# Eight copies of v move from SyncE's to GpSimd's queue, a split of expert weights waits for a gather's issue, and indices are computed before affinities

## The chip, the cores and the metric

The kernel runs on one core of a Trainium2 chip. The metric is the device time of one execution in microseconds (us), the median of several runs. All times in the trace are counted from the start of the profiled execution's span.

## What is computed

A two-layer encoder runs over two sequences, a sample of 512 tokens and a prompt of 256, each of width 1024, in float32. A layer is

```
x = x + token_mixer(rmsnorm(x, norm1), w_in, rpb, gain_na, gain_dil, w_out)
x = x + expert_choice_ffn(rmsnorm(x, norm2), w_router, w_gate, w_up, w_down)
```

The mixer projects x by `w_in` to queries, keys and values of 16 heads of 64. The first four heads are neighborhood attention on a grid of 64 columns: a token of the sample sees 8 rows by 16 columns of keys around it. The other twelve are dilated attention in three patterns. Their outputs are normalised and multiplied by `w_out`.

The feed-forward part is routed by expert choice: `aff = softmax(x @ w_router)`, and each of 16 experts takes its top tokens (64 of the sample, 32 of the prompt), with their affinities `g` and indices `idx`:

```
xe  = x[idx]
ye  = (silu(xe @ w_gate) * (xe @ w_up)) @ w_down * g
y   = zeros.at[idx].add(ye)
```

After two layers a last rmsnorm gives the outputs.

## The kernel before, in words

**Products.** Every large product is made of three products on TensorE: each float32 operand is split into a high part `hi` (rounded by a copy on ScalarE) and a low part `lo` (the rest, a subtraction on VectorE), and hi*hi, hi*lo and lo*hi are summed in PSUM.

**The stream of weights.** `Stream` (L186) loads weights in a fixed order (`prefetch`, L201, a DMA on SyncE's queue, SP, at L209) and splits them in the same order (`convert`, L212: ScalarE's copy at L222 or L225, VectorE's subtraction at L223 or L226, where L222 and L223 are for the query weights, which are scaled). A raw buffer is loaded again when the split that reads it is done: w_in has two raw buffers, the expert weights a ring of 16 quarters of 1 MB.

**The order of the work.** The mixer (`Mixer`) is a set of generators. A planner (`Order` with `Clock`, a cost model of each engine) runs them when the kernel is built and fixes the order in which instructions are put into each engine's queue. Each engine then runs its own queue in order; SP's and POOL's (GpSimd's) queues are such queues too, and a DMA that waits for its data holds up those behind it. The change leaves the planner's costs and the order of the work as they are.

**The start of a layer.** `project` (L765) goes through the units of w_in: first the values of heads 0 to 3, then queries and keys of heads 0 and 1, and so on. The values of a row block of 128 tokens (products L818 to L820) go from PSUM to `y` (L825 on ScalarE, L826 on VectorE). Neighborhood attention of the sample needs v sorted by blocks of 16 columns instead of by rows, so for the first unit the four row blocks of the sample are stored to a DRAM buffer `blocks` (L829, four stores of 256 KB) and, when all four are in DRAM, loaded from it in the other order into `v` (L833, four loads of 256 KB). All eight are issued on SP. Products L788 to L790 are the projections of queries and keys, whose results L755 (ScalarE) and L761 (VectorE) split. L776 clears halves of the key buffers by memsets on GpSimd. L899 and L900 are the scores, L960 and L962 the products with v. `rstd` (L301) takes the power -0.5 on GpSimd (L307). `tables` and `prompt_tables` load attention biases on SP (L849, L856).

**Routing and the first expert.** `choose` finds each expert's top tokens; `choice` (L439) turns them so that each expert is a column and merges two halves: `m` says which half wins, `gT` becomes the affinities, `iT` the indices as integers, `iL` the last expert's indices again. Then `experts` (L316) begins. `gather(e)` (L328) is an indirect DMA on GpSimd (L330) that fetches the 96 rows of expert e from `table` in DRAM by the indices `iT`. Two gathers are issued, a further weight load is made to wait for the second, and `ws.convert(first + 3)` splits the second and third quarter of the first expert's gate weights (the first was split in the mixer). `flip` (L334) turns the gathered rows on TensorE (L340) and splits them (L342 on ScalarE, L343 on VectorE). Then the products run (L357), twelve for each quarter of a weight matrix.

Of the kernel before, what the change touches and what calls it, by code (L numbers as in the profile page):

```python
# [8 lines left out]
F32 = mybir.dt.float32  # L9
# [3 lines left out]
OP = mybir.AluOpType  # L13
# [41 lines left out]
class Clock:  # L55
# [3 lines left out]
    def __init__(self):  # L59
        self.at = dict.fromkeys(("pe", "act", "dve", "pool", "dma"), 0.0)  # L60
# [122 lines left out]
                self.tasks.remove(best)  # L183


class Stream:  # L186

    def __init__(self, nc):  # L190
        self.nc = nc
        self.load, self.parts, self.ready, self.turns = [], {}, {}, {}
        self.loaded = self.split = 0
        self.clock = Clock()
# [17 lines left out]
    def convert(self, n):  # L212
        nc = self.nc
        while self.split < min(n, len(self.load)):
            g = self.split
            while self.load[g][6] is None:
                self.prefetch(self.loaded + 1)
            _, _, size, hi, lo, ahead, w, arrival, _, scale = self.load[g]
            hi = hi([128, size * (1 if lo else 2)], F32R, name="hi")
            hi, lo = (hi, lo([128, size], F32R, name="lo")) if lo else (hi[:, :size], hi[:, size:])  # L220
            if scale:
                nc.scalar.activation(hi, w, AF.Copy, scale=scale)  # L222
                nc.vector.scalar_tensor_tensor(lo, w, scale, hi.bitcast(F32), op0=OP.mult, op1=OP.subtract)  # L223
            else:
                nc.scalar.activation(hi, w, AF.Copy)  # L225
                nc.vector.tensor_sub(lo, w, hi.bitcast(F32))  # L226
            self.ready[g] = self.clock.dve(size, self.clock.act(size, arrival))
            self.parts[g] = (hi, lo)
            self.split += 1
            self.prefetch(g + 1 + ahead)  # L230
# [6 lines left out]
class Kernel:  # L237
    def __init__(self, ctx, tc, a):
        self.tc, self.nc, self.a = tc, tc.nc, a
        nc = self.nc  # L240
        self.mem = ctx.enter_context(tc.tile_pool(name="mem", bufs=1, reuse_waits="tile"))
        self.pp = ctx.enter_context(tc.tile_pool(name="ps", bufs=2, space=bass.MemoryType.PSUM, reuse_waits="tile"))
        self.dram = ctx.enter_context(tc.tile_pool(name="dram", bufs=1, space=bass.MemoryType.DRAM))
        ctx.enter_context(tc.manual_schedule())
        self.zones = {}
        self.const = ctx.enter_context(tc.tile_pool(name="const", bufs=1))
        self.ident = self.const.tile([128, 128], F32, name="ident")
        nc.scalar.dma_start(self.ident, a["ident"])
        self.half = self.const.tile([128, 16], F32, name="half")
        nc.gpsimd.memset(self.half, -0.5)  # L250
        self.gcol = self.const.tile([128, DEPTH, KT], F32, name="gcol")
        nc.gpsimd.dma_start(self.gcol, a["gains"])
        self.wr = self.const.tile([128, DEPTH, KT, EXPERTS], F32, name="wr")
        nc.gpsimd.dma_start(self.wr, a["w_router"])
        g2 = self.const.tile([128, DEPTH, KT], F32, name="g2")
        nc.gpsimd.dma_start(g2, a["norm2_cols"])
        self.g2 = g2
        top = self.region(TOP_AT)
        self.top = top.tile([48, 2, CAP], F32, name="top")
        self.both = top.tile([CAP, 2, 2, EXPERTS], F32, name="both")  # L260
        self.pick = top.tile([CAP, 2, EXPERTS], F32, name="pick")
        self.iota = self.const.tile([CAP, 128], F32, name="iota")
        nc.scalar.dma_start(self.iota, a["iota"])
        self.flip = self.const.tile([CAP, CAP], F32, name="flip")
        nc.scalar.dma_start(self.flip, a["flip"])

        self.half_at = self.const.tile([CAP, 2], F32, name="half_at")
        for s, x in ((slice(0, CAP_S), (SS // 2, SS // 2)), (slice(CAP_S, CAP), (SP // 2, SS + SP // 2))):
            for c in range(2):
                nc.gpsimd.memset(self.half_at[s, c:c + 1], float(x[c]))  # L270
        self.gT = self.const.tile([CAP, EXPERTS], F32, name="gT")
        self.iT = self.const.tile([CAP, EXPERTS], U32, name="iT")
        self.iL = self.const.tile([CAP, 1], F32, name="iL")
        self.xres = self.dram.tile([NTOK, D], F32, name="xres")
        self.table = self.dram.tile([NTOK, D], F32, name="table")
        self.blocks = self.dram.tile([SS, 512], F32R, name="blocks")
        self.ws = Stream(nc)


    def zone(self, name, dtype):  # L280
# [35 lines left out]
    def experts(self, l, first):  # L316

        nc, ws, gT, iT = self.nc, self.ws, self.gT, self.iT
# [44 lines left out]
            return [self.bank(t)[:CAP] for t in tags]  # L363

        gather(0)
        gather(1)
        if ws.loaded < first + len(RING) + 1:
            ws.prefetch(ws.loaded + 1)
            self.tc.add_manual_dep(ws.dma.ins, gathers[1].ins.name, mybir.DependencyInfo(
                mybir.DependencyClass.Sync, mybir.DependencyReason.SCHED_ONLY), reason="rows before more weights")  # L370
            ws.prefetch(first + len(RING) + 1)
        ws.convert(first + 3)
        xT[0] = flip(xe[0], "x")
# [65 lines left out]
    def choice(self):  # L439


        nc, E = self.nc, EXPERTS
        p = self.bank("tp")[:CAP, :128].rearrange("p (v h c) -> p v h c", v=2, h=2)
        for v in range(2):
            nc.tensor.transpose(p[:, v].rearrange("p h c -> p (h c)")[:, :48], self.top[:, v], self.ident[:48, :48])
        t = self.both
        nc.vector.tensor_copy(t, p[:, :, :, :E])
        q = self.bank("tp")[:CAP, :2 * E].rearrange("p (v c) -> p v c", v=2)
        nc.tensor.matmul(q, self.flip, t[:, :, 1], start=True, stop=True)
        self.busy(BUSY[3])  # L450
        m, d = self.pick[:, 0], self.pick[:, 1]
        nc.vector.tensor_tensor(m, t[:, 0, 0], q[:, 0], op=OP.is_ge)
        nc.vector.tensor_tensor(self.gT, t[:, 0, 0], q[:, 0], op=OP.max)
        nc.vector.scalar_tensor_tensor(d, t[:, 1, 0], self.half_at[:, 0:1], q[:, 1], op0=OP.subtract, op1=OP.subtract)
        nc.vector.tensor_mul(d, d, m)
        nc.vector.scalar_tensor_tensor(self.iT, d, self.half_at[:, 1:2], q[:, 1], op0=OP.add, op1=OP.add)
        nc.vector.scalar_tensor_tensor(self.iL, d[:, E - 1:], self.half_at[:, 1:2], q[:, 1, E - 1:], op0=OP.add, op1=OP.add)


# [121 lines left out]
class Mixer:  # L581
# [183 lines left out]
    def project(self):  # L765

        nc, clock, ws = self.nc, self.clock, self.ws
        for n, (kind, i) in enumerate(UNITS):
# [30 lines left out]
            else:  # L799
# [8 lines left out]
                for t in range(TILES):  # L808
                    if t == 2:
                        ws.convert(c + 3)  # L810
                    s = slice(t * 128, (t + 1) * 128)
                    yield lambda: max(self.avail("pj"), ws.ready[c + 1], self.hT_at.get(t, NEVER))
                    hT = self.hT
                    p, b = self.bank("pj")
                    p = p[:, :256]
                    for k, (hi, lo) in enumerate(w):
                        at = clock.pe(768, max(ws.ready[c + 1], self.hT_at[t]))
                        nc.tensor.matmul(p, hT[0][:, k, s], hi, start=k == 0, stop=False)  # L818
                        nc.tensor.matmul(p, hT[0][:, k, s], lo, start=False, stop=False)  # L819
                        nc.tensor.matmul(p, hT[1][:, k, s], hi, start=False, stop=k == KT - 1)  # L820
                        if k < KT - 1:
                            yield lambda: 0.0
                    pv = p.rearrange("p (h d) -> p h d", h=4)
                    y = rows if t < SS // 128 else v
                    nc.scalar.activation(y[:, t, :, 0, :], pv, AF.Copy)  # L825
                    nc.vector.tensor_sub(y[:, t, :, 1, :], pv, y[:, t, :, 0, :].bitcast(F32))  # L826
                    self.free["pj"][b] = at = clock.dve(256, clock.act(256, at))
                    if near and t < SS // 128:
                        nc.sync.dma_start(self.k.blocks[s].bitcast(F32), y[:, t].rearrange("p h a d -> p (h a d)").bitcast(F32))  # L829
                    if near and t == SS // 128 - 1:  # L830
                        src = self.k.blocks.rearrange("(r b c) x -> b r c x", **GRID)
                        for b in range(GRID["b"]):
                            nc.sync.dma_start(v[:, b].rearrange("p h a d -> p (h a d)").bitcast(F32), src[b].bitcast(F32))  # L833
                        blocks_at = clock.dma(2048, at + 2.0)
                if near:
                    at = max(at, blocks_at)
# [503 lines left out]
```

## Time and profile before

| | us |
|---|---|
| median of 3 runs | 2063.65 |
| lowest and highest run | 2063.26, 2066.0 |
| profiled execution | 2064.48 |
| span of the profiled execution | 2062.7 |
| mean granted clock of TensorE | 0.986 |
| TensorE busy | 1983.1 (96% of the span) |
| VectorE, ScalarE, GpSimd busy | 1587.0, 1350.5, 210.7 |

PE is TensorE's matmul, PEld its weight load, DVE is VectorE, ACT ScalarE, POOL GpSimd; a q behind a name is the engine's queue, and SPq is SyncE's. In rows, L226 is line 226 of the kernel, `hi<-data,hi` is what an instruction writes and reads, and `[8.61 <-DVE heads L761]` says that the engine was idle for 8.61 us before it and which instruction ended that. The names are those of memory zones: `heads`, `data`, `turned` and `turned_lo` hold many things in turn. A granted clock of 1.00 is 2.4 GHz, 0.50 is 1.2 GHz.

### The profile page before, as it was taken

How to read it: one execution, taken by the hardware profiler on the slowest of the kernel's cores; microseconds unless marked ns; L12 is line 12 of the kernel's file. 1: busy time of each engine (PE TensorE's matmuls, PEld its weight loads, DVE VectorE, ACT ScalarE, POOL GpSimd, SP SyncE). 2: the span in 40 equal slices, each digit the busy share in tenths (PEclk: the TensorE clock that was granted, in tenths of full speed). 3: DMA queues.
4: the chain of work that ended last, by engine and by line, in shares of the span. 5: the costliest groups of instructions: out<-in, count | busy, mean ns of one | idle time of the engine just before them, and what ended most of it. 6: DMA issues, size and time to landing. Idle time of an engine off the chain costs nothing.

```text
span 2062.7 us, 27876 instructions
## 1 busy us (share of the span) xinstructions
PE 1983.1 (96%) x10602; PEld 1557.3 (76%) x10602; DVE 1587.0 (77%) x1978; ACT 1350.5 (65%) x1743; POOL 210.7 (10%) x149
## 2 busy tenths in 40 slices
PE   6999999989999999999979999999899999999997
PEld 6898898876777777777678998978667777777774
DVE  4566677767888888888846666777688888888887
ACT  4566666427777777777636666663377777777775
POOL 2000000010101010101010000000101010101011
PEclk9999999999999999999989999999999999999999
DMA  6212214679999999999352221246799999999974
GB/s 214 92 57 84 76 57 154 241 235 361 370 389 385 390 385 388 387 386 354 126 171 77 76 79 57 86 181 235 252 346 382 394 377 401 373 397 376 397 283 140
DMA packets 97142, 526.67 MB, mean 255 GB/s; under 512 B 11536, under 2 KB 14864, under 8 KB 47856
## 3 DMA queue, kind: packets, MB, share of 16 engines
q1 hardware_dynamic: 84320, 493.39, 62.8%
q0 software_dynamic: 7200, 25.06, 5.0%
q10 hardware_dynamic: 5488, 6.45, 1.3%
q8 instruction: 83, 1.36, 0.3%
q14 instruction: 51, 0.42, 0.1%
HBM read 485.79 MB, written 32.77 MB: 251 GB/s over the span
## 4 chain that ended last, share of the span: by engine, by line
PE 86%; DVE 5%; ACT 3%; DMA 2%; issue 2%; SPq 0%; ACTq 0%; POOL 0%; POOLq 0%; DVEq 0%
PE pj L357 17%; PE s L357 17%; PE av L357 8%; PE o L357 8%; PE pj L1082 5%; PE pj L788 3%; PE pj L789 3%; PE pj L790 3%; PE tp L932 3%; PE pj L818 2%; PE tp L340 2%; PE pj L820 2%; PE pj L819 2%; PE s L1082 2%; PE av L960 2%
## 5 line engine op out<-in xcount | busy, mean ns | idle before, releaser
L225 ACT ACTIVATE hi<-data 128x2048 fp32r<-128x2048 f32 (+1 forms) x170 | 289.5, 1703 | 61.3 <-PE s L357 24.6
L226 DVE TENSOR_TENSOR hi<-data,hi 128x2048 fp32r<-128x2048 f32 (+1 forms) x106 | 197.9, 1867 | 50.7 <-ACT hi L225 50.1
L357 PE MATMUL pj<-hi,parts 128*96 128x512 f32 x880 | 233.7, 393 | 2.8 <-DVE parts L343 2.3
L357 PE MATMUL s<-turned_lo,parts 128*96 128x512 f32 x872 | 221.7, 393 | 0.0
L908 ACT ACTIVATE data<-data 128x256 f32<-128x256 f32 (+1 forms) x192 | 119.1, 621 | 155.6 <-DVE data L906 147.5
L788 PE MATMUL pj<-turned,hi 128*128 128x256 f32 (+1 forms) x512 | 180.8, 353 | 17.8 <-DVE heads L761 16.5
L357 PEld LDWEIGHTS pj<-hi,parts 128*96 128x96 f32 x880 | 141.6, 161 | 64.7 <-DVE parts L343 3.2
L357 PEld LDWEIGHTS s<-turned_lo,parts 128*96 128x96 f32 x872 | 140.4, 161 | 60.7 <-DVE turned_lo L226 0.4
L357 PE MATMUL pj<-turned_lo,parts 128*96 128x512 f32 x656 | 181.6, 400 | 0.0
L789 PE MATMUL pj<-turned_lo,hi 128*128 128x256 f32 (+1 forms) x512 | 174.6, 341 | 0.0
L790 PE MATMUL pj<-turned,hi 128*128 128x256 f32 (+1 forms) x512 | 174.4, 341 | 0.0
L225 ACT ACTIVATE hi<-heads 128x2048 fp32r<-128x2048 f32 x80 | 152.8, 1913 | 32.4 <-PE s L357 20.4
L226 DVE TENSOR_TENSOR turned_lo<-data,hi 128x2048 fp32r<-128x2048 f32 x64 | 146.7, 2293 | 29.6 <-ACT hi L225 28.2
L357 PE MATMUL s<-hi,parts 128*96 128x512 f32 x664 | 169.0, 392 | 0.0
L226 DVE TENSOR_TENSOR turned_lo<-data,turned_lo 128x2048 fp32r<-128x2048 f32 (+1 forms) x68 | 151.4, 2226 | 19.3 <-ACT turned_lo L225 17.6
L405 POOL DMA_INDIRECT xres<-heads,iT x30 | 53.7, 1791 | 916.6 <-ACT heads L404 916.6
L225 ACT ACTIVATE turned_lo<-data 128x2048 fp32r<-128x2048 f32 (+1 forms) x68 | 127.0, 1868 | 30.0 <-PE pj L357 14.5
L357 PEld LDWEIGHTS s<-hi,parts 128*96 128x96 f32 x664 | 107.1, 161 | 46.3
L937 DVE TENSOR_TENSOR parts<-tp,parts 128x512 fp32r<-128x512 f32 (+2 forms) x160 | 99.6, 647 | 51.0 <-ACT parts L936 49.3
L357 PE MATMUL av<-hi,parts 128*96 128x512 f32 x400 | 134.5, 397 | 3.7 <-DVE hi L226 3.7
L357 PEld LDWEIGHTS pj<-turned_lo,parts 128*96 128x96 f32 x656 | 105.2, 164 | 42.9 <-ACT parts L342 0.5
L906 DVE CUSTOM_DVE_ANT_0 data<-s,data 128x512 f32<-128x512 f32 (+2 forms) x176 | 98.7, 579 | 28.9 <-PE s L900 27.2
(172 smaller groups left out, 4514.7 us busy)
## 6 DMA issues: line engine op xcount, KB each, us to landing
data<-in_w_up SPq DMA_DIRECT2D x70, 1024.0 KB, 8.7
data<-in_w_gate SPq DMA_DIRECT2D x66, 1024.0 KB, 8.1
data<-in_w_down SPq DMA_DIRECT2D x56, 1024.0 KB, 8.9
heads<-in_w_down SPq DMA_DIRECT2D x44, 1024.0 KB, 8.8
heads<-in_w_gate SPq DMA_DIRECT2D x42, 1024.0 KB, 7.6
heads<-in_w_up SPq DMA_DIRECT2D x34, 1024.0 KB, 9.7
turned<-in_w_down SPq DMA_DIRECT2D x28, 1024.0 KB, 8.9
turned<-in_w_up SPq DMA_DIRECT2D x24, 1024.0 KB, 7.0
```

The source lines that it names most:

```text
L225: nc.scalar.activation(hi, w, AF.Copy)
L226: nc.vector.tensor_sub(lo, w, hi.bitcast(F32))
L357: nc.tensor.matmul(ps[b], y[:, k, :], a[:, o:o + 512], start=k == 0 and w == 0, stop=k == KT - 1 and w == 2)
L405: nc.gpsimd.indirect_dma_start(out=self.xres, out_offset=bass.IndirectOffsetOnAxis(ap=iT[:, e:e + 1], axis=0), in_=y, in_offset=None, comp ...
L788: nc.tensor.matmul(p, hi[:, k, :], hT[0][:, k, s], start=k == 0, stop=False)
L789: nc.tensor.matmul(p, hi[:, k, :], hT[1][:, k, s], start=False, stop=False)
L790: nc.tensor.matmul(p, lo[:, k, :], hT[0][:, k, s], start=False, stop=k == KT - 1)
L906: nc.vector.tensor_tensor_reduce(out=x[:, j, :w], in0=p[:, j, :w], in1=tab[:, o:o + w], scale=-1.0, scalar=3.0e38, op0=OP.add, op1=OP.min, ...
L908: nc.scalar.activation(x[:, j, :w], x[:, j, :w], AF.Exp, bias=m, scale=-1.0, accum_out=self.den[n][:, t, a:a + 1])
L932: nc.tensor.transpose(p[:, a * S + t * 128:a * S + (t + 1) * 128], w[:, o:o + 128], self.k.ident)
L937: nc.vector.tensor_sub(lo[:, c], p[:, c], hi[:, c].bitcast(F32))
L1082: nc.tensor.matmul(p, y[:, i], z[:, b * 512:(b + 1) * 512], start=i == 0 and w == 0, stop=i == len(ks) - 1 and w == 2)
```

## The change

The eight copies of v by blocks are issued on GpSimd's queue instead of SP's. After the issue of the first gather GpSimd also clears one element of a new tile `mark`, and the next subtraction of `convert` (L226) has a dependency on that memset, as a wait on a semaphore. `gT` is computed after `iT` instead of right after `m`. The existing dependency between the second gather and a weight load is written by the new helper `order` and stays the same.

```diff
+def order(tc, later, sooner, reason):
+    tc.add_manual_dep(later.ins, sooner.ins.name, mybir.DependencyInfo(
+        mybir.DependencyClass.Sync, mybir.DependencyReason.SCHED_ONLY), reason=reason)
...
                 nc.scalar.activation(hi, w, AF.Copy)
-                nc.vector.tensor_sub(lo, w, hi.bitcast(F32))
+                x = nc.vector.tensor_sub(lo, w, hi.bitcast(F32))
+                if self.behind is not None:
+                    order(self.tc, x, self.behind, "rows asked for before VectorE is busy")
+                    self.behind = None
...
+        self.mark = self.const.tile([1, 1], F32, name="mark")
...
         gather(0)
+        ws.behind = nc.gpsimd.memset(self.mark, 0.0)
         gather(1)
...
         nc.vector.tensor_tensor(m, t[:, 0, 0], q[:, 0], op=OP.is_ge)
-        nc.vector.tensor_tensor(self.gT, t[:, 0, 0], q[:, 0], op=OP.max)
         nc.vector.scalar_tensor_tensor(d, t[:, 1, 0], self.half_at[:, 0:1], q[:, 1], op0=OP.subtract, op1=OP.subtract)
         nc.vector.tensor_mul(d, d, m)
         nc.vector.scalar_tensor_tensor(self.iT, d, self.half_at[:, 1:2], q[:, 1], op0=OP.add, op1=OP.add)
+        nc.vector.tensor_tensor(self.gT, t[:, 0, 0], q[:, 0], op=OP.max)
...
                     if near and t < SS // 128:
-                        nc.sync.dma_start(self.k.blocks[s].bitcast(F32), y[:, t].rearrange("p h a d -> p (h a d)").bitcast(F32))
+                        nc.gpsimd.dma_start(self.k.blocks[s].bitcast(F32), y[:, t].rearrange("p h a d -> p (h a d)").bitcast(F32))
                     if near and t == SS // 128 - 1:
                         src = self.k.blocks.rearrange("(r b c) x -> b r c x", **GRID)
                         for b in range(GRID["b"]):
-                            nc.sync.dma_start(v[:, b].rearrange("p h a d -> p (h a d)").bitcast(F32), src[b].bitcast(F32))
+                            nc.gpsimd.dma_start(v[:, b].rearrange("p h a d -> p (h a d)").bitcast(F32), src[b].bitcast(F32))
```

## Rows read from the trace of the kernel before

**Rows 1.** The page, section 4: engines' shares of the chain that ended last.
```profile
PE 86%; DVE 5%; ACT 3%; DMA 2%; issue 2%; SPq 0%; ACTq 0%; POOL 0%; POOLq 0%; DVEq 0%
```

**Rows 2.** Waits of TensorE, whole span: us in total, times, longest us.
```profile
PE pj L788 <- DVE heads L761: 16.5, 2, 8.6
...
PE tp L340 <- DMA heads<-table,iT: 9.9, 2, 5.3
PE av L357 <- DVE hi L226: 3.7, 2, 1.9
```

**Rows 3.** Timeline of TensorE, layer 0: start, duration, line, names, shapes [idle before].
```profile
37.48 0.40 PE L788 MATMUL pj<-turned,hi 128*128 128x512 f32 x1
...
54.59 0.77 PE L788 MATMUL pj<-turned,hi 128*128 128x512 f32 x1 [8.61 <-DVE heads L761]
...
89.91 0.42 PE L960 MATMUL av<-parts,heads 128*128 128x384 f32 x1
```

**Rows 4.** The chain of waits in order of time, layer 0: start, us, what.
```profile
33.59 5.71 DMA blocks<-heads
...
42.31 8.32 DMA data<-in_w_in
...
66.55 0.47 PE pj L788
```

**Rows 5.** Timeline of VectorE, layer 0.
```profile
24.95 1.23 DVE L223 SCALAR_TENSOR_TENSOR hi<-data,hi 128x1024 fp32r<-128x1024 f32 x1 [0.46 <-ACT hi L222]
...
27.29 1.28 DVE L678 SCALAR_TENSOR_TENSOR data<-data 128x1024 f32<-128x1024 f32 x1
```

**Rows 6.** Stretches: each engine's busy us (instructions), granted TensorE clock, DMA share, GB/s.
```profile
55.00:60.00 5.00, 5.00 (x13) 3.84 (x13) 1.56 (x2) 0.00 (x0) 0.00 (x0) 0.50 0.45 156
```

**Rows 7.** Timeline of TensorE, layer 1.
```profile
1075.76 0.77 PE L788 MATMUL pj<-turned,hi 128*128 128x512 f32 x1 [7.90 <-DVE heads L761]
...
1087.38 0.47 PE L788 MATMUL pj<-turned,hi 128*128 128x512 f32 x1 [0.47 <-ACT heads L755]
```

**Rows 8.** The chain of waits in order of time, layer 1.
```profile
1063.50 8.35 DMA data<-in_w_in
```

**Rows 9.** Timeline of VectorE, layer 1.
```profile
1047.82 1.23 DVE L223 SCALAR_TENSOR_TENSOR hi<-data,hi 128x1024 fp32r<-128x1024 f32 x1 [0.20 <-ACT hi L222]
```

**Rows 10.** Timeline of all engines at the first gather, layer 0.
```profile
451.31 0.23 DVE L456 SCALAR_TENSOR_TENSOR iT<-data,half_at,tp 96x16 uint32<-96x16 f32 x1
...
452.45 4.53 POOL L330 DMA_INDIRECT heads<-table,iT  x1 [11.29 <-issue]
453.78 2.28 DVE L226 TENSOR_TENSOR turned_lo<-heads,hi 128x2048 fp32r<-128x2048 f32 x1
457.29 0.96 POOL L330 DMA_INDIRECT heads<-table,iT  x1 [0.30 <-issue]
...
460.15 1.51 PE L340 MATMUL tp<-ident,heads 96*128 96x96 f32 x8 [4.52 <-DMA heads<-table,iT]
...
465.31 3.39 PE L357 MATMUL pj<-hi,parts 128*96 128x512 f32 x14
```

**Rows 11.** Timeline of all engines at the first gather, layer 1.
```profile
1473.30 4.55 POOL L330 DMA_INDIRECT heads<-table,iT  x1 [11.26 <-DVE iL L457]
...
1481.84 1.51 PE L340 MATMUL tp<-ident,heads 96*128 96x96 f32 x8 [5.33 <-DMA heads<-table,iT]
...
1483.29 4.92 PE L357 MATMUL pj<-turned_lo,parts 128*96 128x512 f32 x12
...
1488.05 3.39 PE L357 MATMUL pj<-hi,parts 128*96 128x512 f32 x14
```

**Rows 12.** The loads of w_in, all 48: from issue to landing.
```profile
DMA to landing us min/median/max: 3.2/4.6/9.0
```

**Rows 13.** Timeline of GpSimd, layer 0.
```profile
23.11 1.46 POOL L307 TENSOR_TENSOR data<-data,half 128x1 f32<-128x1 f32 x1 [1.33 <-DVE data L305]
24.62 3.10 POOL L776 MEMSET heads<- 64x768 f32 x4
```

More of the change, by code (lines that the diff above doesn't have):

```diff
@@ L183, in run, with __init__ @@
                 self.tasks.remove(best)
+def order(tc, later, sooner, reason):
+    tc.add_manual_dep(later.ins, sooner.ins.name, mybir.DependencyInfo(
+        mybir.DependencyClass.Sync, mybir.DependencyReason.SCHED_ONLY), reason=reason)
 class Stream:
-    def __init__(self, nc):
-        self.nc = nc
+    def __init__(self, nc, tc):
+        self.nc, self.tc, self.behind = nc, tc, None
         self.load, self.parts, self.ready, self.turns = [], {}, {}, {}
@@ L276, in __init__ @@
         self.blocks = self.dram.tile([SS, 512], F32R, name="blocks")
-        self.ws = Stream(nc)
+        self.ws = Stream(nc, tc)
     def zone(self, name, dtype):
@@ L368, in experts @@
             ws.prefetch(ws.loaded + 1)
-            self.tc.add_manual_dep(ws.dma.ins, gathers[1].ins.name, mybir.DependencyInfo(
-                mybir.DependencyClass.Sync, mybir.DependencyReason.SCHED_ONLY), reason="rows before more weights")
+            order(self.tc, ws.dma, gathers[1], "rows before more weights")
             ws.prefetch(first + len(RING) + 1)
```

## The prediction

> **What bounds the kernel now.** I read the chain that ended last on the page first: TensorE holds 86% of it [rows 1], so what counts is where TensorE stands still and at which clock it starts again. TensorE's waits over the span say where [rows 2]: two waits of 16.5 us together at L788 (the projection of queries and keys), two of 9.9 us together at L340 (the first turn of gathered rows). The 11.0 us between them is the loading of the input, which the change doesn't touch; no later wait has a sum over 3.7 us. So there are two places in each layer, and the change works at both.
>
> Place one, layer 0. TensorE ends the first query projection and stands from 45.98 to 54.59 (8.61 us) [rows 3]. The chain there [rows 4] goes back from it to a load of w_in that SP issued at 42.31 and that landed 8.32 us later, and from that to SP's wait for the last store of v, issued at 33.59 and landed 5.71 us later: the four loads of `heads<-blocks` wait for the stores, and w_in stands behind them in the same queue. Its buffer was long free: the split that reads it last started at 24.95 and takes 1.23 [rows 5]. After the wait TensorE starts cold: 13 products in 5 us, granted clock 0.50 in 55 to 60 us, the lower level (1.2 GHz) [rows 6]. Layer 1 has the same: 7.90 us before 1075.76 [rows 7], a w_in load issued at 1063.50 that took 8.35 [rows 8], its buffer released by the split at 1047.82 [rows 9].
>
> Place two: after routing, the first gather of token rows. GpSimd's issue of it takes 4.53 us, the second one only 0.96 [rows 10]. During the first, VectorE runs two splits L226, each with two SBUF inputs; the second of these ends at 456.06, and the gather's issue ends 0.92 later, at 456.98. Layer 1 repeats it: 4.55 [rows 11]. So the issue is not long in itself, it is held until VectorE is through. TensorE's turn begins 3.17 us after the end of the issue in layer 0, 3.99 in layer 1. The Trainium skill agrees (GPSIMD Engine Reference, section 1: GpSimd's SBUF interfaces are shared with VectorE, and instructions with two SBUF inputs contend).
>
> **v by blocks on POOL's queue.** Eight copies a layer leave SP for POOL. On SP nothing then stands between the tables and w_in but the wait for its buffer: 26.2 us (24.95 + 1.23) is the earliest issue; 33.6, where SP now issues the last store, is a bound from above. Loads of w_in take 3.2 to 9.0 us to land [rows 12]; with 33.6 + 9.0 it lands at 42.6, with the median 4.6 at 31 to 38. ScalarE's and VectorE's splits follow, 1.2 us each, ahead of the query halves that empty TensorE's bank. TensorE runs 512-column products from 37.48 [rows 3] at 0.23 us, 24 of them to 43.0, and needs the bank at 45.98. It gets it: the 8.6 us go, and with them the cold start. The key projection then takes what the query projection took, 45.98 - 37.48 = 8.5 us, ends at 54.5, and the next unit, 0.5 later as now, begins at 55.0 in place of 66.55 [rows 4]: **11.5 us**. Layer 1: TensorE stops at 1075.76 - 7.90 = 1067.9; + 8.5 + 0.5 = 1076.9 in place of 1087.38 [rows 7]: **10.5 us**. After this TensorE has only the small waits of [rows 2], so the shift is kept.
>
> The price on POOL. An issue there costs between 0.96 (the gather without VectorE) and 4.53 us (with it) [rows 10]; a gain is excluded, since nothing waited for SP's issue time alone. I take 1 to 2, because the splits of this stretch are half as long (1.23). Queued behind the first store is the sixth row block's power, now at 23.11 [rows 13]; its user on VectorE comes at 27.29 [rows 5], so some 2.7 us are free. Behind the four loads, which wait for the stores to land (35 + 2 to 6 us), stand the four memsets of the keys' low halves, now at 24.62 [rows 13]; they would run at about 45 to 48, and the scores that read them come after the key projection, 54.5. The loads themselves land near 50, and are read first by the sample's product at 89.91 [rows 3], then 78: 28 us of cover. With every issue at 4.53 the last load is out at about 62 and landed near 70, still in time. Cost: nothing, and 0 to 2 us at the upper end.
>
> Against this part stands a page. The Trainium skill (DMA: Bandwidth & Descriptors, SWDGE vs HWDGE vs iDMA) says that descriptors of GpSimd's DMAs are written to rings in SBUF, from which VectorE can lock it out, and that DMAs issued by SP are immune. The trace agrees for the gather (4.53 against 0.96). It would make the moved copies later and not the time, since the sum above already pays 4.53 for each.
>
> **The split behind the first gather.** A one-element memset on GpSimd follows the first gather, and the next L226 waits for it. What is queued behind the waiting L226 on VectorE: the second split, then the low halves of the turned rows. The indices end some 0.1 us sooner, since the affinities' maximum no longer stands before them (an estimate: their own step, of the same size, takes 0.23, and such steps overlap) [rows 10]; the gather starts 0.9 after the indices (kept; without VectorE it may be less), so at 452.35, and takes 0.96: 453.3. Splits: 453.5 to 455.7 and to 458.0, TensorE's turn: 453.3 + 3.17 = 456.5 in place of 460.15. In layer 1: 1473.20 + 0.94 + 3.99 = 1478.1 in place of 1481.84. So 3.7 sooner in each. TensorE's idle before it falls from 4.5 and 5.3 us to about 1 and 1.6, so it stays warm. From the first turn to the second quarter's products it needs now 5.16 us (460.15 to 465.31) [rows 10] and 6.21 (1481.84 to 1488.05), where twelve products fill 4.76 [rows 11]. Warm, twelve are 12 x 0.23 = 2.8, the four transposes some 0.4 less: 6.21 - 2.0 - 0.4 = 3.8, and 0.3 for VectorE, whose second split ends at 458.0 as the low halves come up (457.7): 4.1. That is 1.1 and 2.1 us more. Sum: **4.8 and 5.8 us**. What is late next is the second gather, held by both splits to 458.0 + 0.9, that is 0.7 later than now; the second row block, and the w_down loads that wait for it, are needed after eight and sixteen quarters of 2.8 us, so this costs nothing. The second quarter's split (455.7) is ready before 460.5.
>
> Alone, indices before affinities is worth 0.1 us in each layer, counted above.
>
> **Sum.** 11.5 + 10.5 + 4.8 + 5.8 = 32.6 us. The profiled execution took 2064.48 (span 2062.7), 0.8 above the median 2063.65, inside the 2.7 between the runs: 2064.5 - 32.6 = 2031.9, and I say 2032. Bounds: gather 0.6 us sooner in each layer if the 0.9 goes down too, 0.8 less to land in layer 1: 2030; two issues at 1.4, w_in late by 1 to 2 us in a layer: 2037. The case's own range is 2028 to 2038.
>
> **The rivals.**
> The marker marks nothing: the memset is through before the gather's descriptors are written, VectorE starts as now or up to 0.9 later, and the gather's issue still ends 0.92 after the second split. For: nothing in this trace shows a memset right behind a gather. Against: the second gather never starts before the first has ended (457.29 after 456.98) [rows 10]. Price: 10.6 us not won, up to 0.9 lost twice: 2042 to 2044. Chance 0.08.
>
> SP's free time alone is won: the w_in load still meets the block copies in the DMA engines, so it lands sooner only by SP's issuing of them, 42.31 - 39.30 = 3 us for the loads and some 1.3 for the stores. Then half of each wait at L788 stays, and with 4.3 us of idle the cold start too: 2064.5 - 2 x 4.3 - 10.6 = 2045. Against: the copies come 5 to 10 us after w_in now. The Trainium skill (Trainium Kernel Development and Optimization, Key Constraints) has this as a rule: queues of all issuing engines share 16 DMA engines, and issuing from several saves only the sequencer's issue time. Here the row shows a wait of 5.71 us in the queue besides. Chance 0.06.
>
> Slower: POOL becomes the late queue. If VectorE's work of the attention stage holds each load's issue not 4.5 but 12 us, the last is out near 92 and landed near 100, and TensorE waits 22 us for v at its 78 in both layers: 2031.9 + 44 = 2076. It decides from a landing near 94 on, 16 us beyond the 78. Against: VectorE is idle between its instructions there, and no issue in this trace takes over 4.55. Chance 0.05.
>
> No change: the two gains are given back, w_in waiting for something that isn't seen behind SP's wait and the gather held as now: within 4 us of 2064. Chance 0.03.
>
> **Numbers.** The forecast has 0.78. Its range with the marker case and most of SP's case gives 2027 to 2046. A measurement of this kernel tells 0.2% (4 us) from no change: faster 0.92, same 0.03, slower 0.05.
>
> **What would show it.** Right: no TensorE wait over 1 us at L788, clock 1.00 through the key projection, w_in issued before 34 us; the first gather near 1 us long and before both splits, TensorE's turn near 456.5 less the shift of 11.5, granted clock 1.00 after it. Wrong: a wait of TensorE at L960 or L900 for a POOL copy or memset; a first gather of 4 us; the wait at L788 still ending with a landing of w_in.

## The result and the profile after

| | before | after |
|---|---|---|
| median, us (4 runs each) | 2063.89 | 2031.59 |
| lowest and highest | 2063.26, 2066.0 | 2031.25, 2033.3 |
| profiled execution, its span | 2064.48, 2062.7 | 2031.46, 2029.7 |
| mean granted clock | 0.986 | 0.994 |

The ratio is 0.9843, with a 95% interval of 0.9826 to 0.986: 32.3 us less, where 32 was forecast. Line numbers move with the change: L788 is now L797, L340 is L349, L226 is L231, L209 is L214, L330 is L339, L357 is L366, L829 and L833 are L838 and L842, L776 is L785, L899 is L908.

TensorE's waits over the whole span of the kernel after (us in total, times, longest), against [rows 2]:

```profile
PE tp L730 <- DVE data L687: 10.9, 1, 10.9
PE av L366 <- DVE hi L231: 3.7, 2, 1.9
...
PE s L908 <- DMA heads<-heads: 1.8, 2, 1.0
...
PE tp L349 <- DMA heads<-table,iT: 1.1, 1, 1.1
...
PE pj L797 <- ACT heads L764: 1.0, 2, 0.5
```

The 16.5 us at L788 are gone but for twice 0.5, and of the 9.9 us at L340 there is 1.1 left. The trace before has no wait like the 1.8 us at the scores. It can't be put down to the moved copies: two kernels below that keep them on SP have it too (2.2 us with the marker alone, 1.8 with the scalings), and the last kernel below, which has the whole change, has none.

SP's queue at the start of layer 0 (start, duration, line, names), then GpSimd's:

```profile
16.10 0.90 SPq L865 DMA_DIRECT2D last<-in_tab_prompt  x2
17.04 1.38 SPq L858 DMA_DIRECT2D data<-in_tab_na  x3
26.11 23.29 SPq L214 DMA_DIRECT2D data<-in_w_in  x4
```

```profile
24.71 0.59 POOL L838 DMA_DIRECT2D blocks<-heads  x1 [0.21 <-issue]
29.11 0.54 POOL L838 DMA_DIRECT2D blocks<-heads  x1 [3.81 <-DVE heads L835]
33.77 0.54 POOL L838 DMA_DIRECT2D blocks<-heads  x1 [4.12 <-DVE heads L835]
36.63 2.42 POOL L842 DMA_DIRECT2D heads<-blocks  x4 [2.32 <-DMA blocks<-heads]
39.09 3.11 POOL L785 MEMSET heads<- 64x768 f32 x4
```

The first of the four w_in loads leaves at 26.11, where it left at 42.31 [rows 4]: as soon as its buffer is free. The copies cost GpSimd 0.54 to 0.61 us each. The memsets, now behind them, are through at 42.2.

TensorE in both layers, the rows that answer to [rows 4] and [rows 7], and the granted clock during the key projection (columns as in [rows 6]):

```profile
54.94 0.47 PE L797 MATMUL pj<-turned,hi 128*128 128x512 f32 x1 [0.52 <-ACT heads L764]
```

```profile
1061.38 0.47 PE L797 MATMUL pj<-turned,hi 128*128 128x512 f32 x1 [0.47 <-ACT heads L764]
```

```profile
48.00:50.00 2.00, 2.00 (x10) 1.68 (x9) 1.04 (x1) 0.00 (x0) 0.00 (x0) 1.00 0.00 0
```

The first gather in layer 0, all engines, against [rows 10]:

```profile
439.06 6.79 PE L305 MATMUL av<-ident 128*128 128x128 f32 x44
...
439.82 0.23 DVE L464 SCALAR_TENSOR_TENSOR iT<-data,half_at,tp 96x16 uint32<-96x16 f32 x1
...
440.99 1.06 POOL L339 DMA_INDIRECT heads<-table,iT  x1 [11.38 <-issue]
442.05 0.09 POOL L375 MEMSET mark<- 1x1 f32 x1
442.17 2.29 DVE L231 TENSOR_TENSOR hi<-heads,hi 128x2048 fp32r<-128x2048 f32 x1 [1.92 <-POOL mark L375]
442.35 2.94 POOL L339 DMA_INDIRECT heads<-table,iT  x1 [0.21 <-issue]
444.38 2.29 DVE L231 TENSOR_TENSOR turned_lo<-heads,hi 128x2048 fp32r<-128x2048 f32 x1
445.69 0.83 PE L349 MATMUL tp<-ident,heads 96*128 96x96 f32 x8
...
449.62 3.39 PE L366 MATMUL pj<-hi,parts 128*96 128x512 f32 x14
```

And in layer 1, against [rows 11]:

```profile
1445.06 5.16 PE L305 MATMUL av<-ident 128*128 128x128 f32 x44
...
1445.81 0.23 DVE L464 SCALAR_TENSOR_TENSOR iT<-data,half_at,tp 96x16 uint32<-96x16 f32 x1
...
1446.94 1.05 POOL L339 DMA_INDIRECT heads<-table,iT  x1 [11.20 <-DVE iL L466]
...
1451.31 0.85 PE L349 MATMUL tp<-ident,heads 96*128 96x96 f32 x8 [1.10 <-DMA heads<-table,iT]
...
1455.27 3.39 PE L366 MATMUL pj<-hi,parts 128*96 128x512 f32 x14
```

The first gather's issue takes 1.06 us in place of 4.53. The marker is cleared 0.09 us behind it and VectorE starts 0.03 us after that: it marks what it should.

The same five points of both traces add up to the result (sooner is before less after, in us; growth is what it has grown by since the point above):

| point | before | after | sooner | growth | forecast |
|---|---|---|---|---|---|
| layer 0, unit after the first keys | 66.55 | 54.94 | 11.61 | 11.6 | 11.5 |
| layer 0, second quarter's products | 465.31 | 449.62 | 15.69 | 4.1 | 4.8 |
| layer 1, unit after the first keys | 1087.38 | 1061.38 | 26.00 | 10.3 | 10.5 |
| layer 1, second quarter's products | 1488.05 | 1455.27 | 32.78 | 6.8 | 5.8 |
| span | 2062.7 | 2029.7 | 33.0 | 0.2 | |

### The profile page after: what moved, and what is told of

Same layout as the page of the kernel before. It is cut to its first block, busy times and chain, and to the rows that moved or that the text cites. A ratio compares the mean times of both kernels' runs of the same rounds, so it can differ in the third digit from the quotient of the medians.

```text
span 2029.7 us, 27925 instructions
## 1 busy us (share of the span) xinstructions
PE 1974.6 (97%) x10602; PEld 1551.6 (76%) x10602; DVE 1586.8 (78%) x1978; ACT 1349.9 (67%) x1743; POOL 217.3 (11%) x167
## 4 chain that ended last, share of the span: by engine, by line
PE 89%; DVE 5%; ACT 3%; DMA 1%; issue 1%; POOL 0%; ACTq 0%; POOLq 0%; SPq 0%; DVEq 0%
PE pj L366 17%; PE s L366 17%; PE av L366 9%; PE o L366 8%; PE pj L1091 4%; PE pj L797 4%; PE pj L799 4%; PE pj L798 4%; PE tp L941 3%; PE pj L827 2%; PE pj L829 2%; PE pj L828 2%; PE tp L349 2%; PE s L1091 2%; PE s L908 2%; PE av L969 2%
## 5 line engine op out<-in xcount | busy, mean ns | idle before, releaser
L231 DVE TENSOR_TENSOR hi<-data,hi 128x2048 fp32r<-128x2048 f32 (+1 forms) x106 | 197.9, 1867 | 51.2 <-ACT hi L230 50.6
L366 PE MATMUL pj<-hi,parts 128*96 128x512 f32 x880 | 233.8, 393 | 2.8 <-DVE parts L352 2.3
L366 PE MATMUL s<-turned_lo,parts 128*96 128x512 f32 x872 | 221.7, 393 | 0.0
L366 PEld LDWEIGHTS pj<-hi,parts 128*96 128x96 f32 x880 | 141.6, 161 | 64.8 <-DVE parts L352 3.2
L366 PEld LDWEIGHTS s<-turned_lo,parts 128*96 128x96 f32 x872 | 140.4, 161 | 60.7 <-DVE turned_lo L231 0.4
L797 PE MATMUL pj<-turned,hi 128*128 128x256 f32 (+1 forms) x512 | 178.4, 348 | 1.3 <-ACT heads L764 1.0
L366 PE MATMUL pj<-turned_lo,parts 128*96 128x512 f32 x656 | 178.9, 395 | 0.5 <-ACT parts L351 0.5
L799 PE MATMUL pj<-turned,hi 128*128 128x256 f32 (+1 forms) x512 | 172.5, 337 | 0.0
L231 DVE TENSOR_TENSOR turned_lo<-data,hi 128x2048 fp32r<-128x2048 f32 x64 | 146.7, 2292 | 29.6 <-ACT hi L230 28.1
L366 PE MATMUL s<-hi,parts 128*96 128x512 f32 x664 | 169.0, 392 | 0.0
L231 DVE TENSOR_TENSOR turned_lo<-data,turned_lo 128x2048 fp32r<-128x2048 f32 (+1 forms) x68 | 151.4, 2226 | 16.8 <-ACT turned_lo L230 15.0
L366 PEld LDWEIGHTS s<-hi,parts 128*96 128x96 f32 x664 | 107.1, 161 | 46.3
L366 PE MATMUL av<-hi,parts 128*96 128x512 f32 x400 | 134.9, 398 | 3.7 <-DVE hi L231 3.7
L366 PEld LDWEIGHTS pj<-turned_lo,parts 128*96 128x96 f32 x656 | 103.5, 162 | 42.3 <-ACT parts L351 0.9
```

Of the source, the lines that this page charges most:

```text
L231: x = nc.vector.tensor_sub(lo, w, hi.bitcast(F32))
L366: nc.tensor.matmul(ps[b], y[:, k, :], a[:, o:o + 512], start=k == 0 and w == 0, stop=k == KT - 1 and w == 2)
L797: nc.tensor.matmul(p, hi[:, k, :], hT[0][:, k, s], start=k == 0, stop=False)
L799: nc.tensor.matmul(p, lo[:, k, :], hT[0][:, k, s], start=False, stop=k == KT - 1)
```

## The experiments

**v's copies alone and the marker alone.** Two kernels, each with one half of the diff shown above:

> Only the eight copies of v on POOL, no marker, old order of gT and iT. Theory (SP's queue stood in front of w_in): the waits at L788 go in both layers, 11.6 + 10.3 = 21.9 us less than before, 2042. Rival (only SP's issue time is won): w_in some 4 us sooner, half of each wait stays, about 2055.

Measured: 2043.37 against 2064.25, ratio 0.9898 (0.9881 to 0.9915), 20.9 us.

> Marker and order of indices as in the change, v's copies on SP as before. Theory: the first gather's issue about 1 us, 10.6 us less than before, 2053 to 2054. Rival (the marker marks nothing, the gains are all v's): 2064 to 2066.

Measured: 2053.78, ratio 0.9949 (0.9932 to 0.9966), 10.5 us. Together 31.4, and both at once gave 32.3: within the intervals the two parts add up, and each rival that left one of them without effect falls.

**Which copies count.** The next two kernels, made from the kernel before the change, move one kind only:

```diff
-                        nc.sync.dma_start(self.k.blocks[s]...)
+                        nc.gpsimd.dma_start(self.k.blocks[s]...)
```

> Only the four stores of v on POOL, the loads on SP, no marker. Theory (what holds w_in is SP's wait for the stores' landing, which stands in front of the loads): SP still waits, only some 3 us shorter because the tables go out earlier; the wait at L788 stays at 5 to 6 us and the cold start with it, about 2058. Rival (any relief of SP's queue does it): 2042.

Measured: 2058.15, ratio 0.997 (0.9957 to 0.9982), 6.1 us less. SP in layer 0 and TensorE's waits over the span:

```profile
36.48 2.58 SPq L833 DMA_DIRECT2D heads<-blocks  x4
39.17 15.24 SPq L209 DMA_DIRECT2D data<-in_w_in  x4
```

```profile
PE pj L788 <- DVE heads L761: 10.5, 2, 5.9
```

w_in leaves 3.1 us sooner than before, behind the loads still, and 10.5 of the 16.5 us of waiting stay.

```diff
-                            nc.sync.dma_start(v[:, b]...)
+                            nc.gpsimd.dma_start(v[:, b]...)
```

> Only the four loads of v on POOL, the stores on SP, no marker. Theory: SP issues w_in right behind the last store, at 33.9, it lands by 40, in time; all of v's 21.9 us, 2042. Rival (gain in proportion to the issues moved): about 2053.

Measured: 2041.93, ratio 0.9891 (0.9874 to 0.9907), 22.3 us, as much as with all eight. SP in layer 0:

```profile
33.44 0.33 SPq L829 DMA_DIRECT2D blocks<-heads  x1
33.81 15.53 SPq L209 DMA_DIRECT2D data<-in_w_in  x4
```

In the kernel before SP issued the loads here:

```profile
39.36 2.90 SPq L833 DMA_DIRECT2D heads<-blocks  x4
```

So it was the four loads in front of w_in in one queue, and not the number of copies on it: the stores may stay. Of the 8.5 us by which w_in now leaves sooner, 5.4 are the loads' wait for the stores to land and 2.9 their own issue. No run takes away the issue time alone, but 3.1 us sooner, as with the stores moved, won only 6.1 us, so the wait has to go. The Trainium skill (Trainium Kernel Development and Optimization, Key Constraints) states that issuing from several engines only saves the sequencer's issue time. This case does not agree: the four loads have 2.9 us of issue time in a layer, and moving them won 22.3 us in two layers, since their wait in the queue left it with them.

**Indices first, alone.**

```diff
-        nc.vector.tensor_tensor(self.gT, t[:, 0, 0], q[:, 0], op=OP.max)
...
         nc.vector.scalar_tensor_tensor(self.iT, ...)
+        nc.vector.tensor_tensor(self.gT, t[:, 0, 0], q[:, 0], op=OP.max)
```

> The kernel before with iT ahead of gT and nothing else. Theory: 0.1 us a layer, not to be told from no change, 2063.8. Rival (the gather waits for another DVE step, or starts in step with iT but is held anyway): exactly nothing; the trace's distance from iT to the gather tells.

Measured: 2065.55, ratio 1.0004 (0.9994 to 1.0013): no change that can be measured. Its trace, layer 0:

```profile
450.73 0.23 DVE L455 SCALAR_TENSOR_TENSOR iT<-data,half_at,tp 96x16 uint32<-96x16 f32 x1
451.87 4.62 POOL L330 DMA_INDIRECT heads<-table,iT  x1 [11.21 <-DVE iL L457]
```

The gather starts 0.91 after the indices, as before, but its issue takes 4.62 in place of 4.53: it is held to the same point. Without the marker the order is worth nothing at all, by the trace; what it adds to the marker (0.1 us at most) no run here can show.

**The marker one gather later.**

```diff
         gather(0)
-        ws.behind = nc.gpsimd.memset(self.mark, 0.0)
         gather(1)
+        ws.behind = nc.gpsimd.memset(self.mark, 0.0)
```

> The changed kernel with the marker behind the second gather instead of the first. Theory: splits start 1.3 us later, end near 1.3 after the low halves of the turned rows are due, so TensorE's third product waits about 1 us in each layer: 2033 to 2034, and the second gather takes 1 us. Rival (the splits have slack): 2031.6.

Measured: 2034.26, ratio 0.9852 (0.9837 to 0.9867) to the kernel before. The interval overlaps that of the change, so the 2.7 us between them are not shown by the times; the trace shows a part. The second gather, now ahead of the splits, is not held, and TensorE waits for the low halves:

```profile
442.46 0.94 POOL L339 DMA_INDIRECT heads<-table,iT  x1 [0.30 <-issue]
```

```profile
PE pj L366 <- DVE parts L352: 3.7, 4, 1.1
```

In the change the gather takes 2.94 us, and this wait stands at 2.3 us, 2 times. Counted from the indices, the second quarter's products come 0.75 us later than in the change in layer 0 and 1.0 us in layer 1. By the traces, then, the splits have about as little slack as the expectation said, and the marker is better placed behind the first gather.

**GpSimd late.** Three kernels put n powers of 128x16 (5, 2 and 16 of them, some 3 us each) ahead of the four loads in the changed kernel:

```diff
+                        for _ in range(n):
+                            nc.gpsimd.tensor_tensor(self.k.late, self.k.ones, self.k.half, op=OP.pow)
                         for b in range(GRID["b"]):
```

> The changed kernel with five extra powers of 128x16 (about 3 us each) on GpSimd ahead of the four loads. Theory: loads out near 51, memsets done near 55, v landed near 56, all still covered: 2031.6. Rival (POOL's queue has no slack): up to 30 us more, 2060.

Measured: 2038.19, ratio 0.9868 (0.9853 to 0.9884), 6.6 us over the change. Both were wrong: neither nothing nor the rival's 2060. TensorE in layer 0, the stretch after, and the DMAs issued from 52 to 57 us (KB each, median us to landing):

```profile
61.55 0.44 PE L913 MATMUL s<-heads 128*128 128x256 f32 x1 [2.09 <-DMA heads<-heads]
```

```profile
62.00:64.00 2.00, 2.00 (x9) 1.91 (x9) 1.24 (x7) 0.85 (x3) 0.00 (x0) 0.50 0.00 0
```

```profile
heads<-blocks POOLq DMA_DIRECT2D x1, 256.0 KB, 8.5
heads<-heads ACTq DMA_DIRECT2D x2, 128.0 KB, 7.8
```

The key copies in the kernel after, in the same stretch:

```profile
heads<-heads ACTq DMA_DIRECT2D x2, 128.0 KB, 2.2
```

The scores wait for neither v nor the memsets but for the copies of key halves that ScalarE issues at 52 to 56 us. These took 2.2 us to land and now take 7.8, with the loads of v in flight beside them. TensorE waits 2.09 us and starts at granted clock 0.50; in layer 1 it waits 1.79 us and the clock stays at 1.00. The two waits are 3.9 of the 6.6 us; the rest was not taken apart. Whether the meeting in the DMA engines is the cause, and not the queue, was tried with two powers:

> The changed kernel with two powers of 3 us ahead of the four loads. With five of them the loads were in flight together with the copies of the key halves that ScalarE issues from 52 us on. Theory (it was this meeting in the DMA engines that cost 6 us): loads out by 43, landed by 50, nothing lost, 2031 to 2032. Rival (each us on POOL's queue costs its share): 6 us x 6.6/15.4 = 2.6 more, 2034.

Measured: 2031.62, ratio 0.9846 (0.983 to 0.9863). Loads out at 42.8, before the key copies, and nothing is lost. They took 10.5 us to land where 7 were expected, so they were only just landing as the first key copies left at 52.4, and these took 3.3 us.

> The changed kernel with sixteen such powers (about 47 us) ahead of the loads. Theory: the memsets of the keys' low halves, behind the loads, end near 87, and the scores, due at 60, wait 27 us for them in each layer, with a cold start after: 2087 to 2093, slower than before. Rival (only v itself counts, due at 78, landed at 89): 11 us a layer, about 2054.

Measured: 2089.05, ratio 1.0116 (1.0101 to 1.0132), slower than before. TensorE's waits:

```profile
PE s L914 <- POOL heads L788: 52.8, 2, 26.6
```

L788 of that kernel is the memset of the key buffers: the scores wait for it 26.6 us in a layer, as expected, and not for v. Here the loads go out at 82.7, long after the key copies, and these land in 2.2 us again, though GpSimd is busy with powers all the while: by these runs, what the copies met with five powers was the loads.

**What holds the gather's issue.** In the kernel before, the two subtractions beside the first gather (these only; the condition is left out here) become a scaling with one SBUF input:

```diff
-                nc.vector.tensor_sub(lo, w, hi.bitcast(F32))
+                nc.vector.tensor_scalar(lo, w, 0.5, 0.0, op0=OP.mult, op1=OP.add)
```

> The kernel before, but in each layer the two subtractions beside the first gather become a scaling of the raw weights by 0.5 on VectorE, one SBUF input instead of two (the low parts of two weight quarters are then wrong). Theory (an instruction with two SBUF inputs holds GpSimd's issue): first gather's issue 1 to 1.4 us, turn 3 to 4 us sooner and warm, about 2053 to 2055. Rival (any long VectorE instruction holds it): issue until the second scaling's end + 0.9, that is 2.5 to 4.5 us, 2058 to 2064.

Measured: 2059.25, ratio 0.9973 (0.9963 to 0.9982). Layer 0:

```profile
450.28 1.22 DVE L227 TENSOR_SCALAR hi<-heads 128x2048 fp32r<-128x2048 f32 x1
451.15 2.40 POOL L334 DMA_INDIRECT heads<-table,iT  x1 [11.29 <-issue]
451.42 1.22 DVE L227 TENSOR_SCALAR turned_lo<-heads 128x2048 fp32r<-128x2048 f32 x1
453.86 0.96 POOL L334 DMA_INDIRECT heads<-table,iT  x1 [0.30 <-issue]
```

The theory falls, and the issue ends where the rival has it: at 453.55, 0.91 after the second scaling's end at 452.64. This instruction with one input holds the gather as the subtraction with two does, for a shorter time, since it takes 1.22 in place of 2.28 us. But the scaling goes through the same 128x2048 values almost twice as fast, so more than the number of inputs has changed, and "any long VectorE instruction" is not shown: no run has one with a single input at the slow pace.

The store of v issued at 24.71 above took 0.59 us with a split of w_in beside it:

```profile
24.86 1.22 DVE L228 SCALAR_TENSOR_TENSOR hi<-data,hi 128x1024 fp32r<-128x1024 f32 x1 [0.44 <-ACT hi L227]
```

To see whether the splits behind the marker hold plain copies, the last kernel, run once, puts four of them between the marker and the second gather:

```diff
         ws.behind = nc.gpsimd.memset(self.mark, 0.0)
+        for i in range(4):
+            nc.gpsimd.dma_start(self.spare[l][:, 32 * i:32 * i + 32], self.a["ident"][:, 32 * i:32 * i + 32])
         gather(1)
```

> The changed kernel with four plain copies (128x32 each, read by nobody) issued on POOL between the marker and the second gather, so that they meet the two splits. [...] Rival (only the indirect DMA is held, as the stores of v beside L228 suggest): about 0.55 us each. The time is 2031 to 2033 either way.

Measured: 2031.74. Layer 0:

```profile
441.81 2.24 POOL L378 DMA_DIRECT2D spare<-in_ident  x4
441.89 2.29 DVE L231 TENSOR_TENSOR hi<-heads,hi 128x2048 fp32r<-128x2048 f32 x1 [1.92 <-POOL mark L376]
444.10 2.28 DVE L231 TENSOR_TENSOR turned_lo<-heads,hi 128x2048 fp32r<-128x2048 f32 x1
444.35 2.89 POOL L340 DMA_INDIRECT heads<-table,iT  x1 [0.30 <-issue]
```

Four plain issues take 0.56 us each with a split running beside them all the time; the gather behind them takes 2.89, to 0.86 after the second split's end. Beside these subtractions only the indirect DMA is held; no run puts a plain copy beside a scaling.

## Why the prediction was right, and where not

The sum came out nearer than its parts: the growth of the four points is 32.8 us against 32.6, but at the second quarter's products layer 0 fell 0.7 short and layer 1 came 1.0 over. That these cancel is luck; the mechanisms of both gains are those forecast.

**v by blocks** came out as worked: 11.6 and 10.3 us against 11.5 and 10.5, with w_in issued at the earliest point named, the cold start gone (granted clock 1.00) and the unit after it at 54.94 against 55.0. The loads alone carry it.

**The price on POOL** was right as a sum (nothing) and wrong in its parts. An issue costs 0.54 to 0.66 us where the lower bound was 0.96, because the gather was the wrong nearest row: a plain copy's issue is shorter than that of a gather that is free, and beside the splits it is not held. The Trainium skill (DMA: Bandwidth & Descriptors, SWDGE vs HWDGE vs iDMA), which the prediction set against this part, has VectorE lock GpSimd out of the descriptor rings during its 2-port perf mode. The prediction left that condition out and put the gather's 4.53 us down as agreeing; the rows do not name the mode of a VectorE instruction, so neither the held gather nor the free copies test that sentence. And the cover was named wrongly: "28 us of cover" counted to the first read of v, and the memsets were given till 54.5. What is late first is neither: with the loads out from 50 us on they met the key copies in the DMA engines, for 6.6 us in the two layers. So "with every issue at 4.53 the last load is out at about 62 and landed near 70, still in time" would probably have been false; no run has issues that long. The slower rival was right that POOL's queue can turn the sign, and wrong in its place: memsets and scores decide, not v at 78.

**The gather.** The issue fell as worked, the turn came 3.0 us sooner in layer 0 beyond what v's part had brought to the indices (14.46 less 11.49) and 4.2 in layer 1 (30.53 less 26.37), against 3.7. The whole part was 4.2 and 6.4 against 4.8 and 5.8 (the 6.8 of the table holds 0.4 that was already there at the indices). Layer 1 is over by 0.6 mostly because its turn came 3.32 us after the end of the issue in place of 3.99, as the prediction's lower bound allowed. In layer 0 TensorE itself was late: its filler products before the turn (L305, products of the identity that nobody reads) took 6.79 us there and 5.16 in layer 1, so the turn began with no wait for the rows. That is a part of the 0.6: in the last kernel above the fillers of layer 0 took 5.16, TensorE waited for the rows, and the turn came 5.42 us after the indices, where it is 5.64 here and 5.05 in the forecast. The rest is a longer issue and landing. The granted clock had fallen during the fillers:

```profile
441.00:442.00 1.00, 1.00 (x6) 1.00 (x6) 0.00 (x0) 0.00 (x0) 1.00 (x1) 0.50 0.00 0
```

Why it fell there and not in layer 1 is left open. It is not tied to the change: fillers of 6.5 to 6.8 us stand in layer 0 with the marker alone, in both layers with v's copies alone, and in layer 1 with the scalings, which have neither. That both splits would hold the second gather, to 0.7 later than before, was wrong too: it ended at 445.29, 0.83 after the first split's end, while the second split was running. Nothing waited for it, so the sum did not change.

**Indices first** was counted with 0.1 us in each layer; alone it gave nothing.

## What to carry to other kernels

When an engine idles on a late load, look at what stands ahead of the load's issue in its queue: a DMA that waits for another DMA's landing holds up everything behind it, and moving just that one to a queue with nothing urgent behind it gave the whole wait back here, with the cold start of TensorE on top. A copy moved off the critical path still has a place in time: ask what it will meet in the DMA engines and what stands behind it in its new queue, not only when its data is read. Ask for gathered rows before long VectorE work starts, and make that order a dependency.

## What the runs showed that was not expected

- GpSimd's indirect DMA is held in its issue by the VectorE instructions tried beside it (0.96 us free, 4.53 beside two subtractions, 2.40 beside two scalings of 1.22 us); plain DMAs from the same queue are not (0.56 us each beside a subtraction). A memset on GpSimd took 0.09 us right behind the gather.
- The hold lasts through two VectorE instructions for a first gather that starts 0.87 us into the first of them (4.53), and through one for a gather that starts 0.18 us into it (2.94, over 0.83 after that one's end). What makes the difference was not tried.
- 1 MB of copies in flight made copies of 128 KB on another queue take 7.8 us in place of 2.2.
